# A two-layer decoder trunk: routing done row tile by row tile with VectorE's and TensorE's order written by hand, the norm ahead of the experts applied by ScalarE and GpSimd, and one PSUM pool for the whole kernel

## The chip, the core and the metric

The kernel runs on one core of a Trainium2 chip. The core has five engines with a queue of instructions each: TensorE (PE: matrix products into PSUM; PEld is its weight load), VectorE (DVE), ScalarE (ACT), GpSimd (POOL) and SyncE (SP), which here does little but issue transfers from HBM. An instruction starts when those ahead of it on its engine have been issued and the semaphores that it waits on have come. The metric is device time in microseconds (us), the median of the runs.

## What is computed

256 tokens of width 1024 pass through two layers. Each layer is a token mixer (two kinds of causal attention, merged and projected by `w_out`) and a channel mixer, each followed by a residual LayerNorm. The channel mixer of the second layer picks two of eight experts for each token:

```python
def moe_swiglu(x, w_router, w_gate_up, w_down):
    logits = (x @ w_router).astype(jnp.float32)
    top_v, top_i = lax.top_k(logits, TOP_K)
    gates = jax.nn.softmax(top_v, axis=-1)
    combine = jnp.sum(jax.nn.one_hot(top_i, N_EXPERTS, dtype=jnp.float32) * gates[..., None], axis=-2)
    y = jnp.zeros_like(x)
    for e in range(N_EXPERTS):
        y = y + combine[..., e:e + 1].astype(x.dtype) * swiglu(x, w_gate_up[e], w_down[e])
    return y
...
        mix = token_mixer(h, w_in[l], ...)
        h = layer_norm(DEEPNORM_ALPHA * h + mix, ln_mix_g[l], ln_mix_b[l])
```

All data are float32. An expert has 1024 x 7168 weights for gate and up and 3584 x 1024 for down, 44 MB, so the eight experts are some 350 MB of the 451 MB that the kernel reads.

## The kernel before

**Tiles.** The 256 tokens are two row tiles of 128 (t = 0 and 1), the width is 8 blocks of 128 (`KT`) or two halves of 512 (hf). Products keep float32's accuracy by splitting an operand into a high and a low part (`split`, L484: ScalarE writes the high one, VectorE the low one), so `tok` (L452) issues three products for each block.

**From the mixer to the router** (`out_norm` with `routed=True`, L1013). `w_out` comes in four pieces, two for each half. TensorE's order is by hand (L1108): the products of the four pieces for both tiles, and between them, as soon as a half of the sum is there, `turn` (L1092: four transposes of that half, copied by ScalarE) and `choose` (L1100: four small products into the logits). When the last product of a half is issued, `total` (L1040) adds the residual and takes the LayerNorm statistics (`ln_stats`). After that VectorE makes mean and reciprocal deviation of each tile (`ln_scale` L577, a Newton iteration of three rounds, L530) and the logits (L1127, L1128), and applies the norm itself (`ln_apply`, L586: two instructions of 128x512 for each half, L592 and L593). `keep_busy` (L342) fills TensorE's waits with products that nobody reads.

**Routing** (`route`, L1201) is a generator that yields where other work may come between. For both tiles in one go it ranks the eight logits of a token against each other (L1219 to L1229), counts by small products how many tokens ahead of this one chose the same expert (`pb`, L1231), makes from that the place of each token in its expert's list (`posm`, L1233) and, for expert 7 (`FIXED`), a one-hot matrix `hot` of 32 columns (L1237); then it orders the experts by how many tokens they have (`cnt` to `eidi`, L1243 to L1265), and makes the one-hot matrices of the first sorted expert (128 and 64 columns, `one_hots`, L1301).

**Experts** (`moe`, L1617). Expert 7 is known ahead, so its weights are loaded before the routing is done: `ahead` (L428) fills 3 + 6 + 8 + 2 tiles of up to 1 MB (`EXT`, `AHEAD`, `RING`, `MID`). `gather_fixed` (L1311) takes the normed rows of expert 7's tokens by products of `hot` with h, tile by tile and half by half, and ScalarE copies them to `xs` (L1327). Then `plain_job` (L1580) multiplies `xs` with weight tile after weight tile (`aux<-raw,xs`), and each tile that is done gives its buffer to the next load (`slot`, L437). The other seven experts follow in an order set by `merge` (L1676), with their numbers read from `eidi` by SP (`value_load`, L1655). The sums of all experts are normed and stored at the end.

**What sets the order.** A planner orders the instructions of each engine by its own costs, unless a block names the engine in `manual_schedule`: there it keeps the order of the code. In before that holds for TensorE in `out_norm`'s end and the experts' start, and for VectorE in the short block L1132 to L1137. SP issues the loads in one queue. PSUM (8 banks of 128 x 512) is a pool of its own for everything up to the routing (L1860: mm 3, tp 2, aux 2, o 1) and another for the experts (L1634: mm 4, tp 2, aux 2).

Of the kernel before, what the change touches and what calls it, by code (L numbers as in the profile page):

```python
# [33 lines left out]
FIXED = 7  # L34
# [271 lines left out]
class Body:  # L306
# [270 lines left out]
    def ln_scale(self, st):  # L577
# [6 lines left out]
        return mv, self.rsqrt(ve, 1)  # L584

# [427 lines left out]
    def out_norm(self, h, xT, w, nk, g, b, routed=False):  # L1013
# [8 lines left out]
        st = [self.ln_tile() for _ in range(2)]  # L1022
# [6 lines left out]
        def go(i, hf, t, part=None):  # L1029
# [6 lines left out]
            if last and (routed or inner and hf == 0):  # L1036
# [3 lines left out]
        def total(t, hf):  # L1040
            cs = slice(hf * 512, hf * 512 + 512)
            nc.vector.scalar_tensor_tensor(r[t][:, cs], h[t][:, cs], ALPHA, ps[t, hf], op0=OP.mult, op1=OP.add)
            self.ln_stats(r[t], st[t], hf)

# [55 lines left out]
        def choose(t, hf):  # L1100

            for i in range(4):
                self.mm(lgb[:, 8 * t:8 * t + 8], turned[t, hf][:, i * 128:(i + 1) * 128], self.wrg[:, 4 * hf + i],
                        hf + i == 0, hf == 1 and i == 3)
        behind = {1: [(turn, 0, 0)], 2: [(choose, 0, 0)], 6: [(turn, 0, 1)], 7: [(choose, 0, 1), (turn, 1, 0)],
                  8: [(choose, 1, 0)], 9: [(turn, 1, 1), (choose, 1, 1)]}
        spare = self.mm_bank()
        with self.tc.manual_schedule(engines={mybir.EngineType.PE}):  # L1108
            for i in range(3):
                load(*p[i])  # L1110
                go(*p[i], 0, 0)
                go(*p[i], 0, 1)
            load(*p[3])
            for n, (i, part, t) in enumerate(((0, 0, 1), (0, 1, 1), (1, 0, 1), (3, 0, 0), (3, 1, 0), (1, 1, 1), (2, 0, 1), (2, 1, 1), (3, 0, 1), (3, 1, 1))):
                go(*p[i], t, part)
                for f, *x in behind.get(n, ()):
                    if n == 9:
                        self.keep_busy(3, spare)
                    f(*x)
            self.keep_busy(11, spare)  # L1120
        scales = []
        lg = self.rt.tile([128, 2, 8], F32, name="lg")
        for t in range(2):
            mv, rstd = self.ln_scale(st[t])
            scales.append((mv, rstd))
# [815 lines left out]
```

## Time and profile before

| | |
|---|---|
| median of 3 runs | 1432.6 us (1431.32 to 1432.95) |
| the profiled execution | 1429.58 us, of which the span of instructions is 1427.9 us |
| TensorE busy | 1374.9 us, 7936 products |
| VectorE, ScalarE, GpSimd busy | 815.1, 656.6, 17.1 us |
| moved by DMA | 453.46 MB, 317 GB/s over the span read from HBM |
| first product of an expert | 604.12 us after the start of the span |

In the lines of the profile each instruction stands as start, duration, engine, line of the kernel, operation, output<-inputs by the names of their tiles, and its sizes; x2 joins two that follow each other; in brackets stands the idle time of the engine just before and what ended it. SPq is SP's queue of transfers: its row shows when a transfer is issued, not when it lands. A window's line gives, for each engine, the busy time and the number of instructions, then TensorE's granted clock (PEclk, 1.00 is full speed), the busy share of the 16 DMA engines and the rate.

### The profile page before, as it was taken

The page shows a single profiled execution, that of the slowest core. Times are in us where ns is not written, and L with a number is a line of the kernel's source. Part 1 is how long each engine was busy: PE and PEld are TensorE (multiplying, and loading weights), DVE is VectorE, ACT ScalarE, POOL GpSimd, SP SyncE. Part 2 cuts the span into 40 slices and gives each one's busy share as a digit, 9 for nine tenths or more (in the row PEclk, how much of TensorE's full clock was granted, in tenths as well). Part 3 has the DMA queues.
Part 4 walks back from the last instruction along what each step waited for, and adds up shares of the span by engine and source line. Part 5 has one row for each costly group of instructions (what it writes and reads, how often), then busy time and mean ns, then how long its engine had stood idle before and what let it go on. Part 6 is the DMA issues. An engine that isn't in the chain of part 4 may idle for free. (4 is left out here: it accounts for less than half of the span.)

```text
span 1427.9 us, 20834 instructions
## 1 busy us (share of the span) xinstructions
PE 1374.9 (96%) x7936; PEld 932.5 (65%) x7936; DVE 815.1 (57%) x1246; ACT 656.6 (46%) x963; POOL 17.1 (1%) x44
## 2 busy tenths in 40 slices
PE   8999999999989999999999999989999999999996
PEld 6878988888888789755545554456676555544542
DVE  7757778665577678533344443366776635343433
ACT  4667537665356565042333332246664444323320
POOL 4000000000000000000000000000000000000000
PEclk9999999999999999999999999999999999999998
DMA  8834447655375348899999999999999999999996
GB/s 234 266 118 136 162 145 240 198 170 191 104 250 185 118 141 308 351 373 398 391 423 423 420 390 427 426 402 416 404 426 425 427 426 418 426 426 427 425 425 239
DMA packets 137064, 453.46 MB, mean 318 GB/s; under 512 B 8094, under 2 KB 64438, under 8 KB 109564
## 3 DMA queue, kind: packets, MB, share of 16 engines
q1 hardware_dynamic: 136168, 450.99, 81.0%
q0 software_dynamic: 784, 1.05, 0.6%
q8 instruction: 65, 1.06, 0.3%
q14 instruction: 43, 0.35, 0.1%
q10 hardware_dynamic: 4, 0.01, 0.0%
HBM read 450.96 MB, written 1.05 MB: 317 GB/s over the span
## 5 line engine op out<-in xcount | busy, mean ns | idle before, releaser
L486 DVE TENSOR_TENSOR wlo<-raw,whi 128x1024 fp32r<-128x1024 f32 (+2 forms) x456 | 515.0, 1160 | 374.3 <-ACT whi L485 367.8
L485 ACT ACTIVATE whi<-raw 128x1024 fp32r<-128x1024 f32 (+2 forms) x456 | 441.1, 1005 | 351.7 <-DMA raw<-in_w_expert_down 104.0
L340 PE MATMUL mm<-hT,whi 128*128 128x512 f32 x672 | 233.9, 398 | 0.0
L340 PE MATMUL aux<-raw,xs 128*32 128x512 f32 (+3 forms) x1280 | 185.3, 544 | 4.5 <-DMA raw<-in_w_expert_gate_up 4.5
L340 PE MATMUL mm<-hT,wlo 128*128 128x256 f32 x672 | 176.4, 282 | 0.0
L340 PE MATMUL mm<-whi,xh 128*128 128x512 f32 x336 | 140.4, 418 | 10.7 <-ACT whi L485 10.5
L340 PEld LDWEIGHTS mm<-hT,whi 128*128 128x128 f32 x672 | 121.2, 188 | 23.5 <-issue 0.7
L340 PEld LDWEIGHTS mm<-hT,wlo 128*128 128x128 f32 x672 | 126.9, 189 | 9.2 <-issue 2.0
L340 PE MATMUL mm<-whi,xl 128*128 128x512 f32 x336 | 132.6, 395 | 0.0
L340 PEld LDWEIGHTS aux<-raw,xs 128*32 128x32 f32 (+1 forms) x1280 | 56.2, 120 | 105.0 <-issue 97.5
L340 PEld LDWEIGHTS mm<-whi,xh 128*128 128x128 f32 x336 | 63.7, 190 | 61.1 <-ACT whi L485 24.0
L340 PE MATMUL mm<-wlo,xh 128*128 128x512 f32 x336 | 96.7, 396 | 0.9 <-DVE wlo L486 0.7
L340 PE MATMUL mm<-whi,eh 128*128 128x512 f32 x336 | 88.2, 403 | 3.9 <-ACT whi L485 3.9
L340 PE MATMUL aux<-raw,eh 128*32 128x512 f32 (+1 forms) x544 | 87.9, 598 | 4.3 <-DMA raw<-in_w_expert_down 4.3
L340 PEld LDWEIGHTS mm<-whi,eh 128*128 128x128 f32 x336 | 60.0, 188 | 35.8 <-ACT whi L485 17.7
L340 PEld LDWEIGHTS mm<-wlo,xh 128*128 128x128 f32 x336 | 61.7, 188 | 20.0 <-DVE wlo L486 5.5
L340 PEld LDWEIGHTS mm<-whi,xl 128*128 128x128 f32 x336 | 63.8, 190 | 11.2
L481 ACT ACTIVATE sums<-mm 128x512 f32<-128x512 f32 x84 | 50.3, 599 | 28.1 <-PE mm L340 28.1
L340 PE MATMUL aux<-hT,whi 128*128 128x512 f32 x160 | 56.3, 397 | 0.0
L340 PEld LDWEIGHTS aux<-raw,eh 128*32 128x32 f32 (+1 forms) x544 | 23.4, 119 | 50.2 <-issue 44.8
L340 PE MATMUL mm<-raw,xs 128*32 128x512 f32 x448 | 54.9, 592 | 0.0
L340 PE MATMUL mm<-whi,hT 128*128 128x260 f32 (+2 forms) x192 | 50.1, 334 | 0.7 <-ACT hT L527 0.7
(363 smaller groups left out, 1618.1 us busy)
## 6 DMA issues: line engine op xcount, KB each, us to landing
raw<-in_w_expert_gate_up SPq DMA_DIRECT2D x140, 1024.0 KB, 11.8
raw<-in_w_expert_down SPq DMA_DIRECT2D x110, 1024.0 KB, 13.2
raw<-in_w_expert_gate_up SPq DMA_DIRECT2D x112, 768.0 KB, 8.9
raw<-in_w_in SPq DMA_DIRECT2D x36, 1024.0 KB, 6.2
raw<-in_w_ffn_gate_up SPq DMA_DIRECT2D x22, 1024.0 KB, 5.7
raw<-in_w_ffn_down SPq DMA_DIRECT2D x10, 1024.0 KB, 4.9
raw<-in_w_out SPq DMA_DIRECT2D x8, 1024.0 KB, 5.0
raw<-in_w_in SPq DMA_DIRECT2D x8, 520.0 KB
```

The costliest lines, as they stand in the source:

```text
L340: self.made = self.nc.tensor.matmul(out, lhsT, rhs, start=start, stop=stop)
L481: self.nc.scalar.activation(x, bank, AF.Copy, scale=scale)
L485: return (self.nc.scalar.activation(hi, src, AF.Copy), self.nc.vector.tensor_sub(lo, src, hi.bitcast(F32)))
L486: self.nc.vector.tensor_sub(lo, src, hi.bitcast(F32)))
```

## The change

1. The last quarter of `w_out`'s products (tile 1, second half) is cut into two column blocks of 256 (`columns`, `quarter`), and the order of TensorE and VectorE from tile 0's last products to the end of the routing is written by hand.
2. `route` works on one tile at a time (`ranks`, `places`): tile 0 is ranked, counted and its rows of `hot` are made while TensorE is still at tile 1's products; then the same for tile 1.
3. The norm is applied by `ln_aside`: VectorE makes -mean/deviation, ScalarE applies it to each half (128x512), and GpSimd multiplies by g and adds b, in pieces of 256 columns: eight GpSimd instructions for each tile.
4. The gather of expert 7's rows (`gather_half`) starts with tile 0's rows before tile 1's logits exist. The one-hot matrices of the first sorted expert are made later, in `gather`.
5. PSUM is one pool for the whole kernel; the experts' fourth `mm` bank is the bank that was `o`.

```diff
     def banks(self, ctx, name, **banks):
 
-        self.nb = banks
+        self.nb, self.lent, self.turn_of = banks, False, 0
         self.ps = ctx.enter_context(self.tc.tile_pool(name=name, bufs=1, space=bass.MemoryType.PSUM, reuse_waits="tile"))
 
     def mm_bank(self):
+
+        self.turn_of += 1
+        if self.lent and self.turn_of % 4 == 0:
+            return self.o_bank()
         return self.bank("mm", self.nb["mm"])
...
+    def ln_aside(self, r, scale, gb):
+
+        nc = self.nc
+        mv, rstd = scale
+        off = self.keep.tile([128, 1], F32, name="ln_off")
+        nc.vector.scalar_tensor_tensor(off, mv[:, 0:1], -1.0, rstd, op0=OP.mult, op1=OP.mult)
+        for hf in range(2):
+            cs = slice(hf * 512, hf * 512 + 512)
+            nc.scalar.activation(r[:, cs], r[:, cs], AF.Identity, bias=off, scale=rstd)
+            for c in range(0, 512, 256):
+                x = r[:, hf * 512 + c:hf * 512 + c + 256]
+                nc.gpsimd.tensor_mul(x, x, gb[0][hf][:, c:c + 256])
+                nc.gpsimd.tensor_add(x, x, gb[1][hf][:, c:c + 256])
...
-        st = [self.ln_tile() for _ in range(2)]
+        st = [self.keep.tile([128, 4, 6], F32, name="last_st", bufs=2) if routed and t else self.ln_tile() for t in range(2)]
...
-            if last and (routed or inner and hf == 0):
+            if last and (routed and hf + t == 0 or inner and hf == 0):
...
+
+        def quarter(q, whole=False):
+            c = q * 256
+            n = 512 if whole else 256
+            nc.vector.scalar_tensor_tensor(r[1][:, c:c + n], h[1][:, c:c + n], ALPHA, ps[1, q][:, :n], op0=OP.mult, op1=OP.add)
+            for i in range(q, q + n // 256):
+                nc.vector.bn_stats(out=st[1][:, i], in_=r[1][:, i * 256:i * 256 + 256])
 
...
-        behind = {1: [(turn, 0, 0)], 2: [(choose, 0, 0)], 6: [(turn, 0, 1)], 7: [(choose, 0, 1), (turn, 1, 0)],
-                  8: [(choose, 1, 0)], 9: [(turn, 1, 1), (choose, 1, 1)]}
         spare = self.mm_bank()
-        with self.tc.manual_schedule(engines={mybir.EngineType.PE}):
-            for i in range(3):
-                load(*p[i])
-                go(*p[i], 0, 0)
-                go(*p[i], 0, 1)
-            load(*p[3])
-            for n, (i, part, t) in enumerate(((0, 0, 1), (0, 1, 1), (1, 0, 1), (3, 0, 0), (3, 1, 0), (1, 1, 1), (2, 0, 1), (2, 1, 1), (3, 0, 1), (3, 1, 1))):
-                go(*p[i], t, part)
-                for f, *x in behind.get(n, ()):
-                    if n == 9:
-                        self.keep_busy(3, spare)
-                    f(*x)
-            self.keep_busy(11, spare)
-        scales = []
         lg = self.rt.tile([128, 2, 8], F32, name="lg")
-        for t in range(2):
-            mv, rstd = self.ln_scale(st[t])
-            scales.append((mv, rstd))
+        scales = {}
+
+        def logits(t):
+            mv, rstd = scales[t]
             x = self.rt.tile([128, 8], F32, name="lgx", bufs=2)
             nc.vector.scalar_tensor_tensor(x, self.wsum[:, 0:8], mv[:, 0:1], lgb[:, 8 * t:8 * t + 8], op0=OP.mult, op1=OP.add)
             nc.vector.scalar_tensor_tensor(lg[:, t], x, rstd, self.wsum[:, 8:16], op0=OP.mult, op1=OP.add)
-            if t == 0:
-                self.ln_apply(r[t], scales[t], gb, lambda hf: None)
-        routing = self.route(lg)
-        with self.tc.manual_schedule(engines={mybir.EngineType.DVE}):
-            hot = next(routing)
-            self.ln_apply(r[1], scales[1], gb, lambda hf: None, (0,))
-            eidi = next(routing)
-            self.ln_apply(r[1], scales[1], gb, lambda hf: None, (1,))
+
+        def columns(q, pieces):
+            if 0 in pieces:
+                ps[1, q] = self.aux_bank()
+            for i in pieces:
+                self.tok(ps[1, q][:, :256], xT, 4 * i, pcs[i, 1], 1, q * 256 - 512, q * 256 - 256, i == 0, i == 1)
+
+        PE, DVE = mybir.EngineType.PE, mybir.EngineType.DVE
+        with self.tc.manual_schedule(engines={PE}):
+            for x in p[:3]:
+                load(*x)
+                go(*x, 0, 0)
+                go(*x, 0, 1)
+            load(*p[3])
+            go(*p[0], 1, 0)
+            go(*p[0], 1, 1)
+            turn(0, 0)
+            go(*p[1], 1, 0)
+            choose(0, 0)
+        with self.tc.manual_schedule(engines={PE, DVE}):
+            go(*p[3], 0, 0)
+            go(*p[3], 0, 1)
+            total(0, 1)
+            go(*p[1], 1, 1)
+            turn(0, 1)
+            scales[0] = self.ln_scale(st[0])
+            self.ln_aside(r[0], scales[0], gb)
+            quarter(0, True)
+            columns(2, (0,))
+            choose(0, 1)
+            columns(2, (1,))
+            turn(1, 0)
+            columns(3, (0,))
+            choose(1, 0)
+            logits(0)
+            routing = self.route(lg)
             next(routing)
-        return r, (hot, eidi, routing)
+            quarter(2)
+            next(routing)
+            columns(3, (1,))
+            quarter(3)
+            half = self.gather_half(r, next(routing))
+            half(0, 0, (0, 2))
+            self.keep_busy(1, spare)
+            turn(1, 1)
+            half(0, 0, (2, 4))
+            scales[1] = self.ln_scale(st[1])
+            self.ln_aside(r[1], scales[1], gb)
+            choose(1, 1)
+            logits(1)
+            half(0, 1, (0, 4))
+            self.keep_busy(2, spare)
+            next(routing)
+            self.keep_busy(2, spare)
+            half(1, 0, (0, 4))
+            hot, eidi = next(routing)
+            next(routing)
+        return r, (half, hot, eidi, routing)
...
+        def ranks(t):
...
+        def places(t):
+            at = slice(8 * t, 8 * t + 8)
+            V.scalar_tensor_tensor(posm[:, at], pb[:, at], 1.0, sel[:, at], op0=OP.add, op1=OP.mult)
+            V.tensor_scalar(hot[:, t], self.iota[:, 1:SLOTS[FIXED] + 1], posm[:, 8 * t + FIXED:8 * t + FIXED + 1],
+                            None, op0=OP.is_equal)
+        ranks(0)
+        yield
+
+
         pb = self.aux_bank()
-        self.mm(pb[:, 0:16], self.belowb, selb, True, False)
+        self.mm(pb[:, 0:8], self.belowb, selb[:, 0:8], True, True)
+        places(0)
+        yield
+        yield hot
+        ranks(1)
+        self.mm(pb[:, 8:16], self.belowb, selb[:, 8:16], True, False)
         self.mm(pb[:, 8:16], self.onesb, selb[:, 0:8], False, True)
-        V.scalar_tensor_tensor(posm, pb[:, 0:16], 1.0, sel, op0=OP.add, op1=OP.mult)
-        n = SLOTS[FIXED]
-        hot = small("hot", [128, 2, sum(x[3] for x in self.wanted)])
-        for t in range(2):
-            self.hot_last = V.tensor_scalar(hot[:, t, 0:n], self.iota[:, 1:n + 1], posm[:, 8 * t + FIXED:8 * t + FIXED + 1],
-                                            None, op0=OP.is_equal)
         cb = self.aux_bank()
         self.mm(cb[:, 0:8], self.onesb, selb[:, 0:8], True, False)
         self.mm(cb[:, 0:8], self.onesb, selb[:, 8:16], False, True)
-        self.keep_busy(3, self.mm_bank(), self.made)
+        places(1)
...
-        self.one_hots(hot[:, :, n:], self.wanted[1:])
...
+    def gather_half(self, h, hot):
+
+        n = SLOTS[FIXED]
+        xs = self.fixed_rows = self.rt.tile([128, 8, n], F32, name="xs")
         bks = [self.mm_bank() for _ in range(2)]
 
-        def half(t, hf):
-            for i in range(4):
+        def half(t, hf, part):
+            for i in range(*part):
...
-        self.banks(ctx, "experts_ps", mm=4, tp=2, aux=2)
+        self.lent, self.turn_of = True, 0
...
-                self.gather(h, self.wanted[1:], self.mm_bank, first[:, :, SLOTS[FIXED]:])
+                self.gather(h, self.wanted[1:], self.mm_bank)
...
+            self.banks(later, "ps", mm=3, tp=2, aux=2, o=1)
...
-                self.banks(ctx, "dense_ps", mm=3, tp=2, aux=2, o=1)
```

**TensorE between the end of the mixer's products and expert 7.** The rows before: `hot` x `h` are the gathers into `xs` (four products for a half of a tile), `onesb` are products that nobody reads, `aux<-raw,xs` is the first product of expert 7.

```order
L340 MATMUL mm<-hot,h 128x32 x4
L340 LDWEIGHTS onesb
L340 MATMUL mm<-onesb 128x512
L340 MATMUL mm<-hot,h 128x32 x4
L340 LDWEIGHTS onesb
L340 MATMUL mm<-onesb 128x512
L340 MATMUL mm<-hot,h 128x32 x4
L340 LDWEIGHTS onesb
L340 MATMUL mm<-onesb 128x512
L340 LDWEIGHTS onesb
L340 MATMUL mm<-onesb 128x512
L340 MATMUL aux<-raw,xs 32x512 x8
```

And the rows now, from the last product of the mixer on (`tp<-ident,h` are the transposes of tile 1's second half, `o<-wr,rT` its part of the logits, `belowb` begins tile 1's count):

```order
L344 MATMUL aux<-whi,mT_5418 128x256
L344 MATMUL mm<-hot,h 128x32 x2
L344 LDWEIGHTS onesb
L344 MATMUL mm<-onesb 128x512
L1121 MATMUL tp<-ident,h 128x128 x4
L344 MATMUL mm<-hot,h 128x32 x2
L344 MATMUL o<-wr,rT 128x8 x4
L344 MATMUL mm<-hot,h 128x32 x4
L344 LDWEIGHTS onesb
L344 MATMUL mm<-onesb 128x512
```

Tile 0's gathers stand ahead of tile 1's logits now; behind tile 1's count come two idle products, one gather of four (tile 1, first half) and at once the first products of expert 7.

**VectorE once the count is there** (the same place of the routing). Before:

```order
L1284 TENSOR_TENSOR comb<-comb,sel 128x16
L1233 SCALAR_TENSOR_TENSOR posm<-aux,sel 128x16
L1286 TENSOR_REDUCE rt_s<-comb 128x2
L1237 TENSOR_SCALAR hot<-iota,posm 128x32 x2
L1243 COPY cnt<-aux 128x8
L592 SCALAR_TENSOR_TENSOR h<-h,ln_mv,ln_gb 128x512
L1287 RECIPROCAL rt_s<-rt_s 128x2
L593 SCALAR_TENSOR_TENSOR h<-h,rs_y,ln_gb 128x512
L1247 SCALAR_TENSOR_TENSOR key<-cnt,rows 128x8
```

Now, for tile 1 alone:

```order
L1349 TENSOR_TENSOR comb<-comb,sel 128x16
L1351 TENSOR_REDUCE rt_s<-comb 128x2
L1290 SCALAR_TENSOR_TENSOR posm<-aux,sel 128x8
L1352 RECIPROCAL rt_s<-rt_s 128x2
L1291 TENSOR_SCALAR hot<-iota,posm 128x32
L1309 COPY cnt<-aux 128x8
L1353 TENSOR_TENSOR comb<-comb,rt_s 128x16
L1313 SCALAR_TENSOR_TENSOR key<-cnt,rows 128x8
```

The two instructions of the norm are gone from VectorE's row.

**GpSimd**, which had nothing to do here before, now (h_5752 is tile 0, h_5753 tile 1; 5744 and 5746 are the halves of g, 5748 and 5750 those of b):

```order
L1023 MEMSET one_5703 128x128
L601 TENSOR_TENSOR h_5752<-h_5752,ln_gb_5744 128x256 x2
L601 TENSOR_TENSOR h_5752<-h_5752,ln_gb_5746 128x256 x2
L602 TENSOR_TENSOR h_5752<-h_5752,ln_gb_5748 128x256 x2
L602 TENSOR_TENSOR h_5752<-h_5752,ln_gb_5750 128x256 x2
L601 TENSOR_TENSOR h_5753<-h_5753,ln_gb_5744 128x256 x2
L601 TENSOR_TENSOR h_5753<-h_5753,ln_gb_5746 128x256 x2
L602 TENSOR_TENSOR h_5753<-h_5753,ln_gb_5748 128x256 x2
L602 TENSOR_TENSOR h_5753<-h_5753,ln_gb_5750 128x256 x2
```

The planner put all four products of a tile ahead of its four sums, so a tile's first half is done with the sixth of its eight instructions. SP's row changes in one place: two of the first five loads of expert 7 stand ahead of the third piece of `w_out` now and not behind it. On all engines the rows behind the start of expert 7 are the same as before, but for the name of the fourth PSUM bank and for VectorE's later `hot` matrices.

More of the change, by code (lines that the diff above doesn't have):

```diff
@@ L1221, in route @@
-        V.tensor_tensor(eq, eq, self.tri8[:, None].to_broadcast([128, 2, 8, 8]), op=OP.mult)
-        V.tensor_add(gt, gt, eq)
-        rank = small("rank", [128, 2, 8])
-        V.tensor_reduce(rank, gt, axis=AX, op=OP.add)
-        rank = rank.rearrange("p t e -> p (t e)")
-        V.tensor_scalar(selb, rank, 2.0, None, op0=OP.is_lt)
-        V.tensor_scalar(sel, rank, 2.0, None, op0=OP.is_lt)
-        pb = self.aux_bank()
-        self.mm(pb[:, 0:16], self.belowb, selb, True, False)
-        self.mm(pb[:, 8:16], self.onesb, selb[:, 0:8], False, True)
@@ L1233, in route @@
-        V.scalar_tensor_tensor(posm, pb[:, 0:16], 1.0, sel, op0=OP.add, op1=OP.mult)
-        n = SLOTS[FIXED]
-        hot = small("hot", [128, 2, sum(x[3] for x in self.wanted)])
-        for t in range(2):
-            self.hot_last = V.tensor_scalar(hot[:, t, 0:n], self.iota[:, 1:n + 1], posm[:, 8 * t + FIXED:8 * t + FIXED + 1],
-                                            None, op0=OP.is_equal)
+        rank = small("rank", [128, 16])
+        hot = small("hot", [128, 2, SLOTS[FIXED]])
+        def ranks(t):
+            eq, gt = (self.wk.tile([128, 512], F32, name=f"rk{n}", tag=n, bufs=2)[:, :64].rearrange("p (e j) -> p e j", j=8) for n in ("p", "p2"))
+            at = slice(8 * t, 8 * t + 8)
+            lj = lg[:, t, None, :].to_broadcast([128, 8, 8])
+            le = lg[:, t, :, None].to_broadcast([128, 8, 8])
+            V.tensor_tensor(eq, lj, le, op=OP.is_equal)
+            V.tensor_tensor(gt, lj, le, op=OP.is_gt)
+            V.tensor_tensor(eq, eq, self.tri8, op=OP.mult)
+            V.tensor_add(gt, gt, eq)
+            V.tensor_reduce(rank[:, at], gt, axis=AX, op=OP.add)
+            V.tensor_scalar(selb[:, at], rank[:, at], 2.0, None, op0=OP.is_lt)
+            V.tensor_scalar(sel[:, at], rank[:, at], 2.0, None, op0=OP.is_lt)
@@ L1241, in route @@
         self.mm(cb[:, 0:8], self.onesb, selb[:, 8:16], False, True)
-        self.keep_busy(3, self.mm_bank(), self.made)
+        places(1)
         V.tensor_copy(cnt, cb[:, 0:8])
-        yield hot
+        yield
         key = small("key", [128, 8])
@@ L1264, in route @@
         eidi = small("eidi", [128, 8], I32)
-        self.ordered = V.tensor_copy(eidi, eid)
-        yield eidi
+        V.tensor_copy(eidi, eid)
+        yield hot, eidi
         V.tensor_scalar(posm, posm, -1.0, None, op0=OP.add)
@@ L1617, in moe @@
     def moe(self, ctx, h, routing, g, b):
-        first, eidi, routing = routing
+        half, first, eidi, routing = routing
         nc, a, tc = self.nc, self.a, self.tc
@@ L1695, in both_chains @@
             with tc.manual_schedule(engines={mybir.EngineType.PE}):
-                fixed = self.gather_fixed(h, first[:, :, :SLOTS[FIXED]])
+                fixed = self.gather_fixed(half, first)
                 for i in range((RING + EXT + AHEAD + MID + 1) // 2):
```

27 lines of the change are left out of this document (8 added, 19 removed).

## The prediction

> **What bounds the kernel now.** I read the page first, then the windows from the end of the mixer to the middle of the experts, then SP's queue, and then the timeline around expert 7's start, row by row.
>
> ```profile
> PE 1374.9 (96%) x7936; PEld 932.5 (65%) x7936; DVE 815.1 (57%) x1246; ACT 656.6 (46%) x963; POOL 17.1 (1%) x44
> ```
>
> TensorE is busy 96% of the span, but that is an average over stages. The windows show what is short in each (busy time and count of PE, PEld, DVE, ACT and POOL, then the granted clock, the DMA share and GB/s):
>
> ```profile
> 580.00:595.00 15.00, 14.88 (x85) 12.23 (x84) 7.95 (x20) 1.20 (x2) 0.19 (x1) 1.00 1.01 427
> 595.00:600.00 5.00, 4.32 (x29) 2.24 (x27) 3.98 (x23) 1.09 (x3) 0.00 (x0) 1.00 1.01 415
> 600.00:605.00 5.00, 5.00 (x43) 3.49 (x45) 4.81 (x20) 0.28 (x1) 0.00 (x0) 1.00 0.08 34
> 605.00:610.00 5.00, 5.00 (x48) 2.04 (x44) 2.86 (x18) 1.56 (x2) 0.00 (x0) 1.00 0.68 199
> 1100.00:1200.00 100.00, 98.62 (x434) 53.36 (x434) 52.93 (x58) 42.72 (x54) 0.00 (x0) 1.00 1.01 425
> ```
>
> In the experts (1100 to 1200) the DMA engines are full at 425 GB/s: from there on the kernel is a stream of weights, and TensorE follows it. The one hole in that stream is at 600 to 605, where they move 34 GB/s. SP's queue says why:
>
> ```profile
> 541.43 1.52 SPq L434 DMA_DIRECT2D raw<-in_w_expert_gate_up  x3
> 546.06 0.38 SPq L401 DMA_DIRECT2D raw<-in_w_out  x1
> 553.09 0.80 SPq L434 DMA_DIRECT2D raw<-in_w_expert_gate_up  x2
> 554.83 0.38 SPq L401 DMA_DIRECT2D raw<-in_w_out  x1
> 566.01 28.50 SPq L434 DMA_DIRECT2D raw<-in_w_expert_gate_up  x14
> 605.25 38.10 SPq L441 DMA_DIRECT2D raw<-in_w_expert_gate_up  x19
> ...
> SPq L441 <- PE aux L340: 14.4, 8, 10.7
> ```
>
> The last load that needs no used buffer is issued by 594.5; the next waits 10.7 us, until a product of expert 7 has given its buffer back at 605.25. So the end moves with the first product of expert 7, called T here: 604.12 before. What T gains shortens the hole (some 5 us of it), and everything behind is carried along, in the same order on every engine. A gain is worth its length as long as it is shorter than the hole.
>
> What sets T is one chain, tile 1's:
>
> ```profile
> 593.29 0.39 PE L340 MATMUL aux<-whi,mT 128*128 128x512 f32 x1
> 593.71 0.69 DVE L1042 SCALAR_TENSOR_TENSOR h<-h,aux 128x512 f32<-128x512 f32 x1 [2.55 <-PE aux L340]
> 594.44 0.69 DVE L561 BATCH_NORM_STATS2 ln_st<-h 128x6 f32<-128x512 f32 x1
> 595.16 0.21 DVE L581 BATCH_NORM_AGGREGATE ln_mv<-ln_st 128x2 f32<-128x12 f32 x1
> 595.84 0.22 DVE L538 SCALAR_TENSOR_TENSOR rs_q<-rs_y,rs_m 128x1 f32<-128x1 f32 x1
> 596.96 0.22 DVE L1127 SCALAR_TENSOR_TENSOR lgx<-wsum,ln_mv,o 128x8 f32<-128x8 f32 x1 [0.44 <-PE o L340]
> 597.88 0.23 DVE L1128 SCALAR_TENSOR_TENSOR lg<-lgx,rs_y,wsum 128x8 f32<-128x8 f32 x1
> 598.21 0.29 DVE L1219 TENSOR_TENSOR rk_eq<-lg 128x128 f32<-128x128 f32 x1
> 599.66 0.17 DVE L1226 TENSOR_SCALAR selb<-rank 128x16 bf16<-128x16 f32 x1
> 600.33 0.39 DVE L1237 TENSOR_SCALAR hot<-iota,posm 128x32 f32<-128x32 f32 x2
> 600.70 0.74 DVE L592 SCALAR_TENSOR_TENSOR h<-h,ln_mv,ln_gb 128x512 f32<-128x512 f32 x1
> 601.48 0.75 DVE L593 SCALAR_TENSOR_TENSOR h<-h,rs_y,ln_gb 128x512 f32<-128x512 f32 x1
> 602.78 0.97 PE L340 MATMUL mm<-hot,h 128*128 128x32 f32 x8
> 603.79 0.28 ACT L1327 ACTIVATE xs<-mm 128x128 f32<-128x128 f32 x1 [4.48 <-PE mm L340]
> 604.12 1.92 PE L340 MATMUL aux<-raw,xs 128*32 128x512 f32 x16
> ```
>
> From the last product of the mixer (593.29) to T are 10.8 us: sum and statistics, the deviation, the logits, the ranking, `hot` at 600.33, VectorE's norm of tile 1's first half, four gathers from 602.78 and the copy. The other gathers stand between and are done.
>
> **The change part by part.** Loads first. Two of the first five loads of expert 7 go out at about 541.4 and not at 553.09, ahead of two pieces of `w_out`. The bytes are the same. The later pieces land some microseconds later, behind two more loads of 1 MB (2 x 2.5 us at 425 GB/s); the mixer's attention work stands ahead of them on TensorE, so I count 0, and if that cover were gone, up to 5 us. The chance of it is in the rivals. PSUM as one pool removes no wait that the rows show: 0.
>
> Next, the products. The last quarter goes in columns of 256, with twice as many instructions. Their price is in products of that width with new weights for each:
>
> ```profile
> 556.02 0.28 PE L340 MATMUL mm<-yT,wlo 128*128 128x256 f32 x1
> 556.13 0.40 PE L340 MATMUL mm<-yT,whi 128*128 128x256 f32 x2
> 556.37 0.28 PE L340 MATMUL mm<-yT,wlo 128*128 128x256 f32 x1
> ...
> 588.41 0.21 DVE L538 SCALAR_TENSOR_TENSOR rs_q<-rs_y,rs_m 128x1 f32<-128x1 f32 x1
> 588.85 0.22 DVE L538 SCALAR_TENSOR_TENSOR rs_q<-rs_y,rs_m 128x1 f32<-128x1 f32 x1
> ```
>
> Three of them in 0.35 us (556.02 to 556.37), 0.117 each, so twice as many cost what the wide ones did. With the small count products of tile 0 between, and the pipeline's start for each bank, I put the last end an estimated 0.3 later, at about 593.8. Behind it VectorE has 256 columns and not 512: sum and statistics take an estimated 0.40 and 0.37 each (between 0.69 for 512 columns and 0.17 for 16), so the aggregate starts at 594.8 instead of 595.16. The deviation follows alone: 0.68 to the first `rs_q` as before, then three rounds of 0.44 (588.41 to 588.85), so it is there at 596.85. In before the logits could use it only at 597.88, since tile 0's logits and a wait of 0.44 lay between. Tile 0's ranking lies under TensorE's last products, on a VectorE with 7 us free in the 15 of 580 to 595.
>
> The deviation feeds two branches. In the first, logits at about 597.5, ranking on 64 elements and not 128 (four steps shorter by 0.07), the count and `hot` come to about 599.7, which is 0.6 ahead of before. Gathers could begin at 600.0, and four of them with the copy take 1.34 (602.78 to 604.12): T = 601.3 or a little less by this branch, a gain of 2.9.
>
> The second branch is the norm. -mean/deviation is there at 597.05, ScalarE's first half (0.63, the row of its 512-column copies below) at 597.75, and GpSimd starts at 597.8. The first half is done with its sixth instruction, since the order puts all four products ahead of the sums. TensorE's gather of tile 1 waits for it, and behind that wait stand all products of the experts. What one instruction costs is not in the trace, because GpSimd does no arithmetic on two tiles before. The nearest rows:
>
> ```profile
> 561.86 0.63 ACT L987 ACTIVATE mT<-mrg 128x512 fp32r<-128x512 f32 x1 [3.45 <-DVE mrg L983]
> ...
> L617 POOL TENSOR_SCALAR_AFFINE_SELECT uo<-uo 128x256 f32<-128x256 f32 x1 | 0.4, 408 | 0.0
> L617 POOL TENSOR_SCALAR_AFFINE_SELECT ident<-ident 128x128 f32<-128x128 f32 x1 | 0.3, 282 | 0.1
> ...
> 8.96 0.75 DVE L593 SCALAR_TENSOR_TENSOR h<-h,rs_y,ln_gb 128x512 f32<-128x512 f32 x1
> 9.25 0.61 POOL L639 TENSOR_SCALAR_AFFINE_SELECT tri<-tri 128x64 f32<-128x64 f32 x1
> 9.63 0.74 DVE L592 SCALAR_TENSOR_TENSOR h<-h,ln_mv,ln_gb 128x512 f32<-128x512 f32 x1
> ```
>
> A select on 128x256 with one input takes 0.41, the lower end; twice that, 0.82, is the upper, if the second input is read after the first. I take 0.6, the middle, since neither end is nearer. [...]
>
> Then there is VectorE beside it. The select on 128x64 at 9.25 took 0.61, while one of twice the size took 0.28; it lay under two VectorE instructions with two inputs in SBUF each. So I count that GpSimd stands still while VectorE reads two: in this stretch the four ranking instructions of 64 elements, an estimated 0.22 each (0.29 for 128, less 0.07), 0.9 together. [...]
>
> Sixth instruction done: 597.8 + 6 x 0.6 + 0.9 = 602.3. Of the four gathers two need only the first 256 columns, which the fifth instruction completes, so they go ahead; the other two and the copy follow in 1.34 less a little under half of the 0.97 of four, 0.93. T = 603.25, a gain of 0.87. Between the ends of the price, blocked: 0.41 gives T = 602.1 (gain 2.0), 0.82 gives 604.55 (loss 0.4). The second half of the norm lies under the first half's expert products, and the expert numbers for SP come within a microsecond or two of where they did and are used only at the next expert; both 0. Later `hot` matrices are made beside a VectorE half free (2.86 of 5 at 605): 0.
>
> The profiled execution took 1429.58, 3.0 below the median of the runs, 1432.6. 1429.58 - 0.87 = 1428.7; as a median, 1432.6 - 0.87 = 1431.7. I call 0.2%, 2.9 us, about what a measurement of this kernel can tell from no change, so this is none.
>
> **The rivals.**
>
> *GpSimd is not blocked.* Then 0.6 gives T = 602.35 (gain 1.8), a median of 1430.8. For it: the other selects show nothing of blocking, and the 0.61 is one row. Against it: that row is twice its size's price. Chance 0.24.
>
> *GpSimd is quick, `hot` bounds.* At 0.41 or less without blocking the sixth is done by 600.3, and the first branch decides: T = 601.2, gain 2.9, median 1429.7. For it speaks only the 0.41 of the one-input select. Chance 0.12.
>
> *GpSimd is slow, and the kernel slower.* From 597.8 + 6t + 0.9 + 0.93 = 604.12 the change loses if one instruction costs over t = 0.75. At 1.2 (twice 0.6) T is 606.8, a loss of 2.7, median 1435.3. Such a price would also hold up tile 0's gathers, which stand ahead of tile 1's transposes on TensorE. For it: nothing on this GpSimd has two inputs, and each select has a fixed part (0.28 for 128 columns, 0.41 for 256) that eight pieces pay eight times. Against it: eight of 0.6 for tile 0 fit well before 593.8. Chance 0.15, of which 0.07 beyond 0.2%.
>
> *The change doesn't do what it says:* a late piece of `w_out`, or SP held by late expert numbers, takes the gain back; median 1432.6 to 1434. Chance 0.08.
>
> **How the numbers follow.** The forecast, GpSimd's chain with blocking and 0.5 to 0.75 each, has 0.41, and with it 1431.7. The range goes from 1429.0, `hot` bounding and 0.7 for the runs' spread (1431.32 to 1432.95), to 1433.8, an instruction of 0.95; outside lie the far part of the slow case and a little of the quick one. Faster by over 0.2%: the upper part of the quick case, and a little of the unblocked one, 0.12; slower: 0.08; within: 0.80.
>
> **What would show it.** Right: first `aux<-raw,xs` at 602 to 603.5, GpSimd's products and sums in a row of 0.5 to 0.75 each, longer ones beside the ranking, TensorE's idle products ended by the wait for GpSimd, the hole in the DMA shorter by the same time. Wrong: GpSimd over 0.75, the wait before the gather ended by `hot`, a last mixer product after 594.2, a first load of the experts that moves by less than T, or TensorE's granted clock below 1.00 around 600, as idle waits might bring.

## The result, and the profile after

The changed kernel takes 1449.84 us (median of five runs, 1447.70 to 1451.01) against 1431.81 (1431.32 to 1432.95): 1.012 times as long, 95% interval 1.0105 to 1.0135. It is 18.0 us slower, where 0.9 faster was forecast. Its profiled execution took 1449.84, with a span of 1448.1; before's took 1429.58, so the two traces have 20.3 us to explain. Two executions of the runs below (b_off256 at 1546.78, before at 2236.55) went at a mean granted clock of 0.844 and 0.567, where the others show 0.98 to 0.99; the ratios leave them out.

The windows of after at the same places as in the prediction:

```profile
580.00:595.00 15.00, 13.24 (x92) 12.13 (x92) 6.15 (x22) 3.32 (x5) 5.57 (x8) 0.98 1.01 423
595.00:600.00 5.00, 3.93 (x19) 3.74 (x19) 2.57 (x11) 0.00 (x0) 0.00 (x0) 0.50 0.53 221
600.00:605.00 5.00, 3.95 (x27) 3.44 (x26) 3.92 (x15) 2.12 (x3) 1.88 (x3) 0.84 0.88 315
605.00:610.00 5.00, 2.32 (x12) 1.44 (x11) 4.59 (x20) 0.49 (x2) 3.79 (x7) 0.50 0.00 0
1100.00:1200.00 100.00, 96.78 (x417) 53.39 (x417) 54.13 (x55) 46.33 (x56) 0.00 (x0) 1.00 1.01 420
```

Two things are new. Around the routing TensorE's granted clock falls to 0.50, and the hole in the stream of weights is at 605 to 610, later and longer, with a smaller one ahead of it in 595 to 600 (221 GB/s). And far behind it, at 1100 to 1200, where the change touches nothing, the DMA engines are as full as before (1.01) but move 420 GB/s and not 425.

SP's queue, after:

```profile
541.95 2.81 SPq L438 DMA_DIRECT2D raw<-in_w_expert_gate_up  x5
546.58 9.26 SPq L405 DMA_DIRECT2D raw<-in_w_out  x2
566.84 33.00 SPq L438 DMA_DIRECT2D raw<-in_w_expert_gate_up  x14
613.04 39.13 SPq L445 DMA_DIRECT2D raw<-in_w_expert_gate_up  x19
```

The last two of the 14 loads go out at 599.03, where in before they went at 593.71, in both with the end of the mixer's last product (599.00 and 593.68); the smaller hole lies around them. The first buffer is given back at 613.04, 7.8 us later than before (605.25). How much of the 20.3 us that is, and how much lies in the stream, the bytes tell. Moved up to 620 us and from 620 to 1400, before:

```profile
DMA packets 81260, 123.21 MB, mean 199 GB/s; under 512 B 2556, under 2 KB 57876, under 8 KB 79167
...
DMA packets 52629, 325.03 MB, mean 417 GB/s; under 512 B 5369, under 2 KB 5369, under 8 KB 27239
```

and after:

```profile
DMA packets 80699, 120.16 MB, mean 194 GB/s; under 512 B 2502, under 2 KB 57822, under 8 KB 78606
...
DMA packets 52015, 319.96 MB, mean 410 GB/s; under 512 B 5300, under 2 KB 5300, under 8 KB 27594
```

At 620, after is 3.05 MB behind, 7.3 us at 417 GB/s. From there on it loses at 410 against 417: some 330 MB take 805 us and not 791, 14 more. Together 21, which is the 20.3 within the rounding of the rates. So a large part of the loss lies far behind the place that the prediction looked at. (In a_place below, with the buffers back in their old place and T as late, this stretch runs at 415 GB/s: of the 14 us some 10 go with the place of the buffers and 4 with the late start.)

That place, row by row, after. The rows start with tile 0's first transposes, from which I count in all that follows, since the start of this stage moves by up to 5 us from one execution to the next (576.8 to 581.6 in the runs below):

```profile
579.39 0.60 PE L1121 MATMUL tp<-ident,h 128*128 128x128 f32 x4
...
592.28 0.96 PE L344 MATMUL o<-wr,rT 128*128 128x8 f32 x8
593.28 0.22 DVE L1137 SCALAR_TENSOR_TENSOR lgx<-wsum,ln_mv,o 128x8 f32<-128x8 f32 x1 [4.11 <-PE o L344]
593.53 0.77 DVE L1138 SCALAR_TENSOR_TENSOR lg<-lgx,rs_y,wsum 128x8 f32<-128x8 f32 x1
594.41 0.23 DVE L1280 TENSOR_TENSOR rkp<-lg 128x64 f32<-128x64 f32 x1
595.60 0.41 DVE L1066 SCALAR_TENSOR_TENSOR h<-h,aux 128x256 f32<-128x256 f32 x1
596.07 0.17 PE L344 MATMUL aux<-selb,belowb 128*128 128x8 bf16 x1 [2.83 <-DVE h L1066]
598.59 0.41 PE L344 MATMUL aux<-whi,mT 128*128 128x256 f32 x1
603.12 2.77 POOL L601 TENSOR_TENSOR h<-h,ln_gb 128x256 f32<-128x256 f32 x4 [8.84 <-DVE lgx L1137]
603.97 0.64 DVE L1280 TENSOR_TENSOR rkp<-lg 128x64 f32<-128x64 f32 x1
604.53 0.76 DVE L1281 TENSOR_TENSOR rkp<-lg 128x64 f32<-128x64 f32 x1
605.29 0.68 DVE L1282 TENSOR_TENSOR rkp<-rkp,tri 128x64 f32<-128x64 f32 x1
605.86 2.76 POOL L602 TENSOR_TENSOR h<-h,ln_gb 128x256 f32<-128x256 f32 x4
606.01 0.65 DVE L1283 TENSOR_TENSOR rkp<-rkp,rkp 128x64 f32<-128x64 f32 x1
608.29 0.36 DVE L1291 TENSOR_SCALAR hot<-iota,posm 128x32 f32<-128x32 f32 x1
608.80 1.88 PE L344 MATMUL mm<-hot,h 128*128 128x32 f32 x8 [0.34 <-DVE comb L1353]
611.05 3.64 PE L344 MATMUL aux<-raw,xs 128*32 128x512 f32 x16 [0.37 <-ACT xs L1387]
```

Three things go wrong here. VectorE waits 4.11 us for tile 0's logits, until the small products of tile 1's first half (592.28) are done too; TensorE then waits 2.83 for tile 0's count, which stands ahead of its last twelve products; and those run at a granted clock of 0.50 (595 to 600), the last at 598.59. Later, beside GpSimd, each of four steps of tile 1's ranking takes 0.64 to 0.76 where the same step of tile 0 took 0.23 with GpSimd idle (594.41). GpSimd's own instructions take 0.69 there (2.77 and 2.76 for four) and 0.70 to 0.71 for tile 0 (2.83 and 2.78 for four, from 588.71 on), where VectorE waited for most of that time.

From the first transposes T, the first product of expert 7, came 25.55 us later before and 31.66 after, and the first buffer back 26.68 and 33.65.

### The profile page after: what moved, and what is told of

Read it like the earlier page. It is cut to its first block, busy times and chain, and to the rows that moved or that the text cites. A ratio compares the mean times of both kernels' runs of the same rounds, so it can differ in the third digit from the quotient of the medians.

```text
span 1448.1 us, 20886 instructions
## 1 busy us (share of the span) xinstructions
PE 1382.3 (95%) x7942; PEld 936.7 (65%) x7942; DVE 816.3 (56%) x1251; ACT 660.0 (46%) x967; POOL 28.3 (2%) x60
## 3 DMA queue, kind: packets, MB, share of 16 engines
q0 software_dynamic: 784, 1.05, 0.5%
HBM read 450.96 MB, written 1.05 MB: 312 GB/s over the span
## 5 line engine op out<-in xcount | busy, mean ns | idle before, releaser
L344 PE MATMUL mm<-whi,xh 128*128 128x512 f32 x256 | 107.9, 422 | 11.0 <-ACT whi L489 10.8
L344 PE MATMUL mm<-whi,xl 128*128 128x512 f32 x256 | 102.0, 398 | 0.0
L344 PE MATMUL mm<-wlo,xh 128*128 128x512 f32 x256 | 81.9, 403 | 0.8 <-DVE wlo L490 0.7
L344 PEld LDWEIGHTS mm<-whi,xh 128*128 128x128 f32 x256 | 48.7, 190 | 45.9 <-issue 19.0
L344 PE MATMUL mm<-whi,eh 128*128 128x512 f32 x224 | 66.7, 409 | 5.4 <-ACT whi L489 5.2
L344 PEld LDWEIGHTS mm<-whi,eh 128*128 128x128 f32 x224 | 38.5, 188 | 33.3 <-ACT whi L489 23.6
L344 PEld LDWEIGHTS mm<-wlo,xh 128*128 128x128 f32 x256 | 47.8, 189 | 17.9 <-DVE wlo L490 4.9
L344 PEld LDWEIGHTS mm<-whi,xl 128*128 128x128 f32 x256 | 48.8, 191 | 9.0
L344 PE MATMUL mm<-raw,xs 128*32 128x512 f32 x384 | 47.3, 592 | 0.0
```

The costliest lines, as they stand in the source:

```text
L344: self.made = self.nc.tensor.matmul(out, lhsT, rhs, start=start, stop=stop)
```

## The experiments

Theory, once the traces were read: two causes that have nothing to do with each other. First the memory. `ln_off` takes two slots of 32 bytes in the pool `keep`, so everything allocated behind that pool moves up by 64: in the built programs the ring of eight weight buffers of the experts starts at byte 23040 of a partition before (90 x 256) and at 23104 after, and a load into a buffer that starts there is slower. Second the routing, through the wait for tile 0's count, the clock behind it, and VectorE held by GpSimd. Rivals: the stream is slow for another reason (the order of the loads, or TensorE's phase); the routing's loss is GpSimd's alone.

| kernel | median us | ratio to before, 95% | hot | T | first buffer back |
|---|---|---|---|---|---|
| before | 1431.81 | | 21.76 | 25.55 | 26.68 |
| after | 1449.84 | 1.0105 to 1.0135 | 28.90 | 31.66 | 33.65 |
| b_off64 | 1442.49 | 1.0049 to 1.0083 | 21.75 | 25.54 | 26.67 |
| b_off128 | 1438.97 | 1.0040 to 1.0068 | 21.75 | 25.55 | 26.67 |
| b_off256 | 1433.10 | 0.9996 to 1.0016 | 21.76 | 25.55 | 26.68 |
| a_align | 1439.27 | 1.0027 to 1.0060 | 28.43 | 31.06 | 33.05 |
| a_place | 1439.93 | 1.0037 to 1.0063 | 29.59 | 32.22 | 34.21 |
| a_align_early | 1437.31 | 1.0025 to 1.0053 | 22.10 | 25.64 | 27.63 |
| a_place_early | 1434.51 | 1.0003 to 1.0025 | 22.09 | 25.64 | 27.63 |
| a_early_ve | 1432.71 | 0.9994 to 1.0012 | 21.05 | 25.14 | 27.14 |
| a_early_ve_busy | 1433.37 | 0.9998 to 1.0019 | 22.05 | 25.40 | 26.53 |
| a_whole | 1433.15 | 0.9991 to 1.0013 | 21.11 | 25.21 | 27.20 |
| a_whole_busy | 1430.36 | 0.9979 to 1.0002 | 21.09 | 24.35 | 25.48 |
| b_aside | 1432.43 | 0.9996 to 1.0022 | 21.96 | 26.83 | 28.83 |

Each ratio is to runs of before on the same chip (their medians lie between 1431.8 and 1432.6). The last three columns are starts in the profiled execution, in us from tile 0's first transposes: tile 1's (before: the first) `hot`, T, and the issue of the first load that waited for expert 7.

**The ring's place, by itself.** Three kernels are before with one line more, ahead of the experts' ring (16, 32 or 64 floats: 64, 128 or 256 bytes):

```diff
+                ctx.enter_context(self.tc.tile_pool(name="gap", bufs=1)).tile([128, 16], F32, name="gap")
                 self.weights_in(ctx, "experts_w", RING, PW)
```

> The kernel before, with only a gap of 64 bytes put ahead of the ring of eight weight buffers of the experts, so that each buffer starts 64 bytes past a multiple of 512, as in the changed kernel. Theory (the misplaced ring makes every load into it a little slower): the DMA rate of 1100 to 1200 falls from 425 to about 420 GB/s, the time rises by 10 to 13 us, to about 1443; T stays at 604.1. Rival (the slower stream after the change comes from the order or the phase of TensorE and the loads, not from the addresses): no difference, 1432.

> The same with a gap of 256 bytes. If what counts is a start at a multiple of 256, no difference, 1432. If it has to be 512, the same rise as with 64 bytes, about 1443. Rival (addresses don't matter): 1432 too.

> The kernel before with a gap of 128 bytes ahead of the experts' ring, where 64 cost 10 us and 256 about 1. Theory (only a start at a multiple of 256 is free, and every other one costs the same): 420 GB/s in 1100 to 1200, 1441 to 1444. Rival (a multiple of 128 is enough): 426 GB/s, 1432 to 1434.

The experts at 1100 to 1200 with 64 bytes:

```profile
1100.00:1200.00 100.00, 98.72 (x424) 54.26 (x424) 54.39 (x55) 45.80 (x55) 0.00 (x0) 1.00 1.01 420
```

and with 256, where the loads that go ahead of the routing are seen as well:

```profile
580.00:595.00 15.00, 15.00 (x86) 12.91 (x85) 6.71 (x18) 1.80 (x3) 0.19 (x1) 1.00 0.32 117
...
600.00:605.00 5.00, 4.42 (x33) 2.96 (x32) 4.62 (x23) 0.49 (x2) 0.00 (x0) 1.00 1.00 423
1100.00:1200.00 100.00, 98.64 (x429) 53.55 (x430) 53.47 (x57) 43.86 (x55) 0.00 (x0) 1.00 1.01 426
```

64 bytes cost 10 us and slow the stream to 420 GB/s with every engine's instructions in the same order; 256 cost nothing that can be told. The theory holds and the rival falls. 128 bytes give 420 GB/s as well, as forecast, but cost 7.1, less than the forecast 1441 to 1444; whether that is less than what 64 cost stays open, since the intervals overlap, but a multiple of 128 is not enough. A gap moves the experts' working tiles behind the ring as well. The work that reads the ring is not what is slower: from 1000 to 1400 us the splits of 128x1024 take 1.05 us on ScalarE and 1.22 on VectorE both in before and in after (ring at 23104), while the DMA engines, as full as ever (1.01), move 420 GB/s and not 425. Each gap also makes a buffer of the ring overlap two of the mixer's buffers, so that some loads go out later: the hole in the stream moves from 600 to 605 into 580 to 595 (117 GB/s), and with 256 bytes the time stays the same. In the kernels with a gap, then, T does not end the hole: with 256 bytes T is at 606.40, and the engines are full from 595 on.

Four places have been measured, then: 23040 (425 GB/s) and 256 bytes further (426) are fast, 64 and 128 bytes further are slow (420), 1.2 to 1.4% less. What in a load takes longer there, no run shows.

**The ring put back in the changed kernel**, once with a gap of 448 bytes, once by keeping -mean/deviation in a third column of the tile that holds the mean, so that each address of the ring is that of before:

```diff
-        mv = self.keep.tile([128, 2], F32, name="ln_mv")
-        nc.vector.bn_aggr(out=mv, in_=st)
+        mv = self.keep.tile([128, 3], F32, name="ln_mv")
+        nc.vector.bn_aggr(out=mv[:, 0:2], in_=st)
...
-        off = self.keep.tile([128, 1], F32, name="ln_off")
+        off = mv[:, 2:3]
```

> The changed kernel, with a gap that puts the experts' ring back to multiples of 512; the routing is left as it is. Theory (two causes: the place of the ring, about 12 us, and the routing, which ends 7 to 8 us later): 425 GB/s in 1100 to 1200, T at 611, 1438 to 1441. Rival (the stream is slow for another reason): 1449 to 1450.

> The changed kernel, with -mean/deviation kept in a third column of the mean's tile instead of two tiles of its own, so that the ring of weight buffers lies where it lay before; nothing else is changed. Theory (two causes): the stream is back at 425 GB/s in 1100 to 1200, the first product of expert 7 stays at about 611, and the time falls by 10 to 13 us, to 1437 to 1440. Rival (the gap that the last aligned kernel put in helped for another reason, since it also moved the loads that wait for the mixer's buffers): 1445 or more.

```profile
1100.00:1200.00 100.00, 97.40 (x424) 53.68 (x424) 53.39 (x54) 47.05 (x57) 0.00 (x0) 1.00 1.01 426
```

This is a_place: the stream is back at 426 GB/s with T as late as ever (32.22), and the time falls by 9.9 us. Ten of the eighteen microseconds were two tiles of four bytes in each partition. a_align falls by about as much, but it is the less clean test, since its gap also moves the hole.

**Tile 0 routed early** (on top of each of the two), in the block that orders TensorE and VectorE by hand:

```diff
             choose(0, 1)
+            logits(0)
+            routing = self.route(lg)
+            next(routing)
             columns(2, (1,))
             turn(1, 0)
             columns(3, (0,))
             choose(1, 0)
-            logits(0)
-            routing = self.route(lg)
-            next(routing)
             quarter(2)
```

> As the one before, and tile 0's logits, ranking and count are written ahead of tile 1's first transposes, so that VectorE waits for the first tile's products into the bank o alone and not for the small products of tile 1 as well. Theory (TensorE stood 2.83 us ahead of the last columns for tile 0's count, and its clock was halved behind that): no such wait, granted clock 1.00 in 595 to 600, the last column at about 593.8, T at 606 to 607.5, 3 to 5 us faster than the aligned kernel without it, 1434 to 1437. Rival (the whole loss of the routing is VectorE waiting for GpSimd; the wait of TensorE is hidden): T at 610 or later, within 1 us of the aligned kernel.

> The same, and tile 0's logits, ranking and count written ahead of tile 1's first transposes. Theory: no wait of 2.8 us for the count, T at 604.5 to 606, but the first product of expert 7 still at half clock; 1433.5 to 1436.5. Rival (the wait was not on the path): within 1 us of the kernel without it.

Both tiles' logits lie in one bank, and in after VectorE's reader of tile 0's, which stands behind tile 1's small products in the code, waited 4.11 us, until they were done (592.28). With the reader ahead of tile 1's products the wait of 2.83 is gone (0.2 in a_place_early), the last product of the mixer comes 15.45 after the transposes and not 19.20, and T 6.6 sooner (25.64). With the ring in its old place (a_place) the time falls by 5.4, to 1434.51; the wait was on the path. With the gap (a_align) T comes 5.4 sooner as well, but the time falls by 2.0 only, to 1437.31, just outside its forecast, and the two intervals overlap. The hole tells why. The same window in a_align and in a_align_early:

```profile
580.00:595.00 15.00, 15.00 (x102) 13.64 (x100) 4.62 (x16) 3.31 (x5) 4.09 (x6) 1.00 0.03 6
...
580.00:595.00 15.00, 14.82 (x108) 13.75 (x106) 9.56 (x29) 3.27 (x5) 5.62 (x8) 1.00 0.16 54
```

Here the DMA engines move at most 5 GB/s from 580 to 590 in both kernels and are full again (1.00 to 1.02) from 600 to 615, ahead of T (612.64 and 604.90), and in the 40 us from the transposes on 11.1 MB are moved in both: T ends no hole, so an earlier T shortens none. What is left in a_place_early:

```profile
596.00:600.00 4.00, 2.94 (x23) 1.92 (x22) 3.56 (x16) 1.90 (x4) 2.00 (x3) 0.69 0.97 391
600.00:604.00 4.00, 2.74 (x14) 1.98 (x16) 3.83 (x15) 0.28 (x1) 3.65 (x7) 0.50 0.07 29
```

```profile
600.24 0.57 DVE L1291 TENSOR_SCALAR hot<-iota,posm 128x32 f32<-128x32 f32 x1
600.74 2.10 POOL L602 TENSOR_TENSOR h<-h,ln_gb 128x256 f32<-128x256 f32 x3
601.51 1.14 PEld L344 LDWEIGHTS mm<-hot,h 128*128 128x128 f32 x5 [1.80 <-POOL h L602]
```

Now the gather waits for GpSimd, whose fifth instruction ends at 601.44, the wait that the prediction had put on the path; and the clock is 0.50 again: the first sixteen products of expert 7 take 3.64 (1.92 in before), and the first buffer comes back 2.0 after T (1.1 before).

**Tile 1's norm on VectorE again**, as before the change (`ln_apply` of the first half behind `hot`, of the second behind `eidi`):

> The same with tile 1's norm back on VectorE, as before the change (two instructions of 128x512 for a half, the first half behind the matrix hot); tile 0's stays with ScalarE and GpSimd. Theory (while GpSimd reads two tiles, a VectorE instruction with two tiles in SBUF waits until GpSimd's is done, some 0.45 to 0.55 us each time): the ranking of tile 1 takes 0.22 a step in every step, hot comes about 1.5 us sooner, but VectorE then needs 1.5 us for the norm: T at 603 to 605, 1432 to 1435. Rival (what GpSimd does beside VectorE costs nothing): the norm's 1.5 us come on top, T at 606 or later, 1435 or more.

```profile
600.39 0.21 DVE L1283 TENSOR_TENSOR rkp<-rkp,tri 128x64 f32<-128x64 f32 x1
602.16 0.74 DVE L610 SCALAR_TENSOR_TENSOR h<-h,ln_mv,ln_gb 128x512 f32<-128x512 f32 x1
602.93 0.75 DVE L611 SCALAR_TENSOR_TENSOR h<-h,rs_y,ln_gb 128x512 f32<-128x512 f32 x1
603.74 1.92 PE L344 MATMUL mm<-hot,h 128*128 128x32 f32 x8 [1.16 <-DVE h L611]
```

Without GpSimd beside it a ranking step takes 0.21 and `hot` comes 1.0 sooner. VectorE then has the norm's 1.5 to do, and T is still 0.5 sooner, at 25.14; the time, 1432.71, is no different from before's, nor clearly from a_place_early's, since the intervals overlap. What the norm on GpSimd frees on VectorE it takes back through VectorE's slower routing and the gather's wait.

**Idle products against the falling clock.**

> The same with 3, 6 and 6 idle products of TensorE in the three waits of tile 1's routing, where there were 1, 2 and 2. Theory (TensorE's clock falls to half when it waits for some 2 us in all): granted clock 1.00 from 595 to 610, the gathers and the first products of expert 7 at full speed, T 0.5 to 1 us sooner and the first buffer given back another 0.9 sooner: 1431 to 1433. Rival (the clock falls for another reason, or the idle products only delay what waits): no faster than without them.

The rival was right: it is no faster (1433.37 against 1432.71), with T 0.3 later and the first buffer back 0.6 sooner. In this kernel, TensorE by timeline and window:

```profile
599.81 1.06 PE L344 MATMUL mm<-hot,h 128*128 128x32 f32 x8
600.71 2.02 PE L344 MATMUL mm<-onesb 128*128 128x512 bf16 x6
```

```profile
600.00:604.00 4.00, 4.00 (x22) 2.06 (x22) 3.05 (x17) 0.49 (x2) 0.20 (x1) 0.68 0.01 4
```

TensorE counts as busy all the time and the clock falls nonetheless. What stands ahead of that are small products, of 8 and 32 columns; and at the lower clock the six idle ones take 2.02 and hold up tile 1's count by about 1.0 (`hot` at 22.05, not 21.05). So the next try put them among the small ones.

**The last quarter in 512 columns**, and then idle products between the gathers as well:

```diff
-            columns(2, (0,))
+            go(*p[2], 1, 0)
...
-            quarter(2)
             next(routing)
-            columns(3, (1,))
-            quarter(3)
+            go(*p[3], 1, 1)
+            quarter(2, True)
```

> The changed kernel with the ring in its old place, tile 0 routed early, tile 1's norm on VectorE, and now the last quarter of the mixer's products in 512 columns again, as before the change. Theory (the columns of 256 cost TensorE some 0.12 us for every 12 products and a later end, 1.6 us in all from tile 0's sum to the last product: 10.7 against 9.1): the last product starts 9.1 to 9.4 after tile 0's sum, the first product of expert 7 19.1 to 19.6 after it (20.37 with columns), 1431 to 1432.5. Rival (the late end comes from the count that stands among the products, not from their width): the last product stays at 10.5, no gain.

> The same with idle products of 512 columns not only in the waits but also between the small products of the routing (3 ahead of tile 1's last transposes, 2 ahead of the gather of tile 0's second half and 3 behind it, 7 behind tile 1's count). Theory (the clock falls when TensorE does little for some 3 us, and products of 8 and 32 columns count as little): granted clock 1.00 throughout 595 to 610, the first buffer given back 1.1 and not 2.0 us behind the first product of expert 7; 1430 to 1431.5. Rival (the idle products delay as much as the clock gains, as in the kernel with 3, 6 and 6): within 0.7 us of the kernel without.

By itself the width gives 0.54 to the last product (14.91 after the transposes, with columns 15.45) and nothing to T, since sum and statistics behind it then take 0.69 and 0.75 (in columns 0.42 and 0.43). My expectation of 1.6 was counted from tile 0's sum, which itself came 0.9 earlier in all kernels with the new order (4.77 and not 5.65). Of the 0.19 that is left against before (14.72), 0.08 is the count: from the small products ahead of it to the next wide one it is 0.89, in before 0.81. With the idle products among the gathers:

```profile
596.00:600.00 4.00, 3.62 (x29) 2.89 (x27) 3.54 (x20) 1.09 (x3) 0.00 (x0) 1.00 0.40 170
600.00:604.00 4.00, 2.94 (x24) 1.70 (x26) 3.70 (x19) 0.28 (x1) 0.20 (x1) 1.00 0.00 0
604.00:608.00 4.00, 4.00 (x36) 1.75 (x40) 3.46 (x17) 1.06 (x2) 0.00 (x0) 1.00 0.48 134
```

The clock holds at 1.00 although TensorE waits more than with 3, 6 and 6 (busy 2.94 of 4 us at 600 to 604, there 4.00), T is 24.35 and the first buffer is back 25.48 after the transposes, 1.2 sooner than in before. The median is 1430.36, the ratio 0.9979 to 1.0002: the best of all versions, and not told apart from before or from a_whole.

**The norm alone**, put on before: `ln_aside` for both tiles in place of `ln_apply`, with the mean's third column, nothing else.

> The kernel before, with nothing of the change but the norm on ScalarE and GpSimd for both tiles. Theory (GpSimd's eight instructions of 0.69 stop VectorE's two-tile instructions, and the gather of tile 1 waits for the sixth): a ranking step beside GpSimd takes 0.6 to 0.8 and not 0.29, hot is 0.5 to 1.5 us later than before, VectorE saves 1.5 us ahead of the gather, and T is 20.0 to 21.5 after tile 0's sum where it was 19.9: 1432 to 1434. Rival (a norm off VectorE is worth its 1.5 us): T at 18.5 to 19, 1430.5 to 1431.

```profile
601.12 0.29 DVE L1233 TENSOR_TENSOR rk_gt<-rk_gt,rk_eq 128x128 f32<-128x128 f32 x1
601.20 2.84 POOL L597 TENSOR_TENSOR h<-h,ln_gb 128x256 f32<-128x256 f32 x4 [3.77 <-ACT h L594]
602.64 1.45 DVE L1248 TENSOR_SCALAR hot<-iota,posm 128x32 f32<-128x32 f32 x2
603.55 1.05 PE L340 MATMUL mm<-hot,h 128*128 128x32 f32 x8 [0.56 <-DVE hot L1248]
604.01 2.76 POOL L598 TENSOR_TENSOR h<-h,ln_gb 128x256 f32<-128x256 f32 x4
```

T is 1.3 later. The last of the ranking's four long steps starts at 601.12, just ahead of GpSimd, so other than forecast they are not slowed (0.28 to 0.29 each); `hot`, 0.39 for two in before, takes 1.45 beside GpSimd, and the first gather waits 0.56 for it. The time cannot be told from before's (0.9996 to 1.0022). The norm on GpSimd by itself is worth between 0.6 us gained and 3.2 lost.

## Why the prediction was wrong

- **What bounds the kernel.** The hole in the stream and T as its end held in every kernel without a gap. This step failed: "everything behind is carried along". The order behind T is the same, but the stream itself became slower by 1.2%, and by the medians that is the larger part, 9.9 us of 18.0. No term of my sum stood for where buffers lie, though the diff showed a new tile in `keep`.
- **Loads.** Counted at 0; with all else put right (a_early_ve) no loss is left for them to carry. Right as far as the runs show.
- **One PSUM pool.** Counted at 0 and not tried by itself. What is left over in a_early_ve, within 0.12%, holds it.
- **The products in columns.** 0.3 later forecast. (The sum slips there: 0.3 behind before's last end, 593.68, is 594.0 and not 593.8.) Without the wait it is 0.73, of which 0.54 is the width and 0.19 the new order with its count. The start for each bank, which I counted into the 0.3, is shown by no run; what the runs show is the 0.73. From the last product's end to the deviation 3.05 us were counted, and it took 3.0 (599.00 to 602.00).
- **"Tile 0's ranking lies under TensorE's last products."** This step failed too. The count stands in TensorE's row ahead of the last twelve products, its bank comes free only when VectorE has read the column block before, and that reading stands behind a ranking that waits for tile 1's small products. I looked at whether VectorE had time, and not at who waits for it. With the clock it costs 5.4 us of the median (a_place to a_place_early).
- **The clock** stood in the list of what would make the forecast wrong, and did: 0.50 at 595 to 600 and at 605 to 610. So did two others of that list: the last mixer product came at 598.59, and the gather waited for `hot`.
- **GpSimd's price.** 0.6 forecast, 0.69 measured. In the changed kernel the gather waited for `hot` and not for GpSimd; with tile 0 early it does wait for GpSimd (1.80 in a_place_early).
- **Who blocks whom.** I let GpSimd stand still for VectorE, 0.9 us. It was the other way round: GpSimd keeps its 0.69 to 0.71, and VectorE's four ranking steps took 2.73 together where 0.22 each was expected, 1.85 more. GpSimd's rows stand end to end (603.12 to 608.62), so that each of the four began while one of GpSimd's ran; and each ended some 0.1 after one of GpSimd's, an estimate that parts the 2.77 and 2.76 for four evenly. That looks like a wait of VectorE each time; for what, no run shows. The row at 9.25 of before, from which I took the direction, was one row.
- **The sum.** 9.9 (the ring's place), 5.4 (tile 0 late), 1.8 (tile 1's norm on GpSimd) take 1449.84 to 1432.71, before's time. They are differences of medians from one kernel to the next, so they have to add up; the 1.8 is not clear of the noise, and T accounts for 0.5 of it.

## What to carry to other kernels

Where a kernel lives on a stream of loads, look at the addresses that a change moves, too: a few bytes ahead of a ring of buffers cost about as much here as all reordering (9.9 and 8.1 us). When an order is written by hand, follow for each instruction on the bounding engine what stands ahead of its producer on the other engine, and which bank it waits for. And a helper engine that reads tiles beside VectorE was not free of charge on VectorE's side here: four ranking steps took 2.73 us beside it and 0.89 without.

## What the runs showed of the hardware that was not expected

- The rate of the loads went with the place where the ring starts in a partition: at 1100 to 1200 us 425 to 426 GB/s at 23040 (before, a_place), 256 bytes further (b_off256) and at 23552 (a_align), 420 at 64 (after, b_off64) and 128 bytes further (b_off128), at the same busy share of 1.01.
- Beside GpSimd's instructions of two tiles, VectorE's `TENSOR_TENSOR` of 128x64 takes mostly 0.64 to 0.78 instead of 0.22; the compare with one tensor input (`hot`) takes 0.36 to 0.57 instead of 0.24, and two of them 1.45 instead of 0.39 in b_aside; GpSimd's do not get longer (four take 2.76 to 2.85).
- The granted clock fell to 0.50 within a wait of 2.83 us (after: 1.00 at 593 to 594, then 0.72 and 0.50), and also where TensorE counted as busy without a gap from 599 on, but up to 600.7 with products of 8 and 32 columns (a_early_ve_busy: 1.00 to 601, then 0.73 and 0.50). With wide products between the small ones it stayed at 1.00 from 590 to 612 (a_whole_busy). How long TensorE has to do little before the clock falls is measured by no run; the 2 and 3 us of two expectations are estimates that none pins down.
